# Hybrid SSD and short-convolution step: rows of x and B through VectorE transposes and DRAM, and a new order of the units in a group

## The chip, the cores and the metric

The kernel runs on one core of a Trainium2 chip. The metric is the time of one execution on the device in microseconds (us), as the median of three runs. Beside the timed runs there is one execution taken with the hardware profiler; its page and its trace are what is read here. Engines are named as in the profile: PE is TensorE (PEld its weight loads), DVE is VectorE, ACT is ScalarE, POOL is GpSimd, SP is SyncE, which here only issues DMAs.

## What is computed

One decoder layer for 336 tokens: 16 meta tokens and 256 prompt tokens in one sequence, and eight sample sequences of eight tokens. Cut to what matters here:

```
h = rms_norm(x);  proj = h @ w_in            # 2048 columns in, z | x,B,C | dt | four short-conv parts | two gates
x, B, C = silu(causal_conv4(proj[x,B,C]))    # x: 64 heads of 64; B, C: 8 groups of 128
cb = einsum('bcign,bcjgn->bcijg', C, B)      # per chunk of tokens i, j and group g
wts = cb[..., None] * decay * dt
y  = einsum(wts, x) + einsum(C, h_in) * exp(acum) + d_skip * x
chunk_states = einsum('bcjgr,bcjgrp,bcjgn->bcgrpn', to_end, x, B)    # then carried from chunk to chunk
y  = grouped_rms_norm(y * silu(z));  y_a = y @ w_ssd_out
y_b = (sc_b * conv3(sc_c * sc_h) * silu(sc_z)) @ w_sconv_out
out = x + (sigmoid(g_a) * y_a + sigmoid(g_b) * y_b) @ w_o            # then a final rms_norm
```

Everything is float32. The outputs are the normed tokens and the new convolution and scan states.

## The kernel before

Activations lie transposed: a tile has 128 features on the partitions and the tokens along the free axis. To keep float32 precision every operand of a large product is split into a high and a low part (`whi`, `wlo` for weights, `hhi`, `hlo` for activations, `yh`, `yl` for the scan's output), and a product is three matmuls: high by high (L111), high by low (L112) and low by high (L115), in `mm`. `wblk` (L90 to L97) loads 128x1024 weights into `wraw` by a DMA on SP's queue (L92), makes `whi` on ScalarE (L94) and `wlo` on VectorE (L96); each of the three tiles has three buffers. A unit is one 128-wide output tile with its two weight blocks (`unit`, `proj`), or, in `out_units`, one weight block for two output tiles. The result stands in a PSUM tile `pj`, of which there are two, until ScalarE or VectorE has emptied it.

The first part of the kernel does the short convolution branch and prepares tables (`dtt`, `act`, `tet`, decays and so on). The last part is the output projection. Between them stand eight groups g of the SSD branch, each of eight heads. Four kinds of units belong to a group:

- `conv_units` (L481 to L494): the projection and convolution of B, of C and of four x tiles. `conv_tile` (L457 to L479) copies `pj` into a padded tile on ScalarE (L462, L463), mends the sequence borders on POOL (L464 to L466), and convolves in the tile `cacc` (L469 on ScalarE, three times L471 on VectorE, L474 on ScalarE, L475 and L476 on VectorE). They are run one group ahead, for g+1.
- `z_units` (L496 to L506): four projections of z, emptied by ScalarE (L502, L503).
- `out_units` (L733 to L745): eight units of y @ w_ssd_out, run one group behind, for g-1. Each unit's two tiles are added into `ya` by VectorE (L744); for g = 0 ScalarE copies them (L742).
- `gate_units` (L747 to L763): the gates, four of them in group 0, four in group 7, the rest behind.

The scan itself, `ssd(g, st)`, is a generator with 24 steps. Its chunks c are 128, 128 and 80 tokens. `rows(c)` (L530 to L552) brings what the scan needs with tokens on the partitions: four TensorE transposes of the x tiles (L534) and one of B (L536) into PSUM, the C.B product (L537), then xdt = rows of x times dt (L539), the high and low part of B's rows (L546, L547; L542 for c = 2), and the masked C.B product `cbm` (L551). `decay` and `weights` make the matrix W from the table rows in DRAM (loaded at L527), the masked product and xdt; `halve`, `carry` and `state` carry the state; step 13 multiplies W by xdt (L650) and collects the scan's output in `ys`; later steps multiply by z (L673), take the group norm (L698 to L705), update the sample states (`h`, L713, L716, written back at L719) and scale `ys` and split it into yh and yl (L726 to L728).

`weave` (L775 to L786) sets the order. It goes through the units in the order of `parts`, each with a weight, and after each unit advances `ssd` so far that the 23 steps spread evenly over the weights. Program order is priority: the instructions of a step stand after those of the unit before them, and `behind` holds them, on ScalarE, VectorE and TensorE, behind the latest weight split or matmul of that unit. The compiler then arranges each engine's queue by this priority and by when it expects operands to be ready. Before, a group's order is z (4 units of weight 2), the output units of g-1 (8 of weight 1), the gates in groups 0 and 7 (4 of weight 2), and the convolutions of g+1 (6 of weight 2).

Two buffers limit the order. The tile `free` (L517), which holds B's rows of chunk 1 and the split xe, takes the slot that the x tiles of g+1 are written to later. And `yh`, `yl` have one buffer each, which the output units of g-1 read; `zq` (L692) uses yh's slot.

Of the kernel before, what the change touches and what calls it, by code (L numbers as in the profile page):

```python
# [1 line left out]

# [11 lines left out]
P = 128  # L14
T = 336
# [14 lines left out]
NSTEP = 23  # L30

# [16 lines left out]
def tile_hybrid_step(ctx, tc, xT, w0, w1, w2, wdt, wso, wsc, wo, cmask, vec, hvec, convst, sconvst, xe_, fwe, h0T,  # L48
# [13 lines left out]
    bq_d = [dr.tile([80, 4, P], F32, name=f"bq_d{i}") for i in range(2)]  # L62

# [26 lines left out]
    def wblk(src, n=1024):  # L90
        raw = wp.tile([P, 1024], F32, name="wraw")
        nc.sync.dma_start(raw[:, :n], src)  # L92
# [5 lines left out]

    def behind(tail):
        for ins in reversed(nc.cur_bb.bb.instructions):  # L100
            if ins is tail:
                break
            for a in latest.values():
                if ins.engine == a.engine:
                    tc.add_manual_dep(ins, a.name, mybir.DependencyInfo(mybir.DependencyClass.NoSync,
                                                                         mybir.DependencyReason.DATA), reason="step")
# [341 lines left out]
    with tc.tile_pool(name="pb", bufs=2) as pb:  # L448
# [8 lines left out]
        def conv_tile(src, j, t0, out, cs):  # L457
# [11 lines left out]
            nc.scalar.activation(acc[:, i0:], pad[:, i0:360], AF.Identity, bias=col(V_CB, j), scale=col(V_CW, 4 * j))  # L469
            for k in range(1, 4):  # L470
                nc.vector.scalar_tensor_tensor(acc[:, i0:], pad[:, i0 + k:360 + k], col(V_CW, 4 * j + k),  # L471
                                               acc[:, i0:], mult, add)
# [6 lines left out]
                acc[:, 272:360].rearrange("p (b t) -> p b t", t=11)[:, :, 3:11], add, mult)  # L479

        def conv_units(g, st):  # L481
            cs = pb.tile([P, 6, 9, 3], F32, name="cs")
            nc.sync.dma_start(cs, convst[:, g])
            BT = st["BT"] = pb.tile([P, T], F32, name="BT")
            conv_tile(w1[64 + g], 32 + g, 0, BT, cs[:, 4])
# [5 lines left out]
            for t in range(4):  # L491
                conv_tile(w1[32 + 4 * g + t], 4 * g + t, 0, xs[:, t, :], cs[:, t])
                yield
            nc.sync.dma_start(convo[:, g], cs)  # L494

        def z_units(g, st):  # L496
            st["zs"] = []
            for t in range(4):
# [4 lines left out]
                nc.scalar.activation(z[:, :TV], pz, AF.Copy)  # L503
                nc.vector.scalar_tensor_tensor(z[:, :TV], th, 1.0, z[:, :TV], add, mult)
# [9 lines left out]
        def ssd(g, st):  # L514
# [6 lines left out]
            W, xdt, xe, bt, cbm, hst = ([None] * 3 for _ in range(6))  # L521
# [8 lines left out]
            def rows(c):  # L530
                (t0, n), m = CH[c], NT[c]
                pp = ps.tile([P, 512], F32, name="ms")
                for t in range(4):
                    nc.tensor.transpose(pp[:n, t * P:t * P + P], xs[:, t, t0:t0 + n], ident)  # L534
                pq = ps.tile([P, 512], F32, name="ms")
                nc.tensor.transpose(pq[:n, 0:P], BT[:, t0:t0 + n], ident)  # L536
                nc.tensor.matmul(pq[:n, P:P + m], BT[:, t0:t0 + n], CT[:, TGT[c]:TGT[c] + m], start=True, stop=True)  # L537
                xdt[c] = big("xdt", 3)
                nc.vector.tensor_tensor(split(xdt[c][:n]), split(pp[:n]), bc(hv(dtt[:n, c, :], g), [n, 8, HP]), mult)  # L539
                if c == 2:  # L540
                    bt[c] = pb.tile([P, P], F32, name="bt", bufs=1)
                    nc.scalar.activation(bt[c][:n], pq[:n, 0:P], AF.Copy)  # L542
                else:
                    bt[c] = (free[:, 1024:1280].rearrange("p (i n) -> p i n", n=P) if c else
                             pb.tile([P, 2, P], F32R, name="bh0", bufs=1))
                    nc.scalar.activation(bt[c][:, 0, :], pq[:, 0:P], AF.Copy)  # L546
                    nc.vector.tensor_tensor(bt[c][:, 1, :], pq[:, 0:P], fb(bt[c][:, 0, :]), sub)  # L547
                cbm[c] = pb.tile([P, PX], F32, name="cbm")
                u0 = META if c == 0 else 0
# [486 lines left out]
```

## Time and profile before

| | us |
|---|---|
| median of 3 runs | 1823.05 (1822.67 to 1823.65) |
| the profiled execution | 1824.75, of which 1823.0 from the first to the last instruction |
| PE busy | 1814.9 |
| DVE busy | 1147.7 |
| ACT busy | 828.8 |
| POOL busy | 389.4 |

The granted TensorE clock is 1.00 throughout. The DMA engines moved 331.33 MB. In the timeline the groups begin after some 696 us and end at about 1645 us; a group in the middle takes 111.4 us. In rows of grouped instructions, the numbers behind the bar are the busy time in us, the mean length of one in ns, and then the engine's idle time just before them. In a timeline the first number is the start in us, the second the duration. A matmul's duration overlaps the next one's; the distance from start to start tells what it costs.

### The profile page before, as it was taken

The page shows a single profiled execution, that of the slowest core. Times are in us where ns is not written, and L with a number is a line of the kernel's source. Part 1 is how long each engine was busy: PE and PEld are TensorE (multiplying, and loading weights), DVE is VectorE, ACT ScalarE, POOL GpSimd, SP SyncE. Part 2 cuts the span into 40 slices and gives each one's busy share as a digit, 9 for nine tenths or more (in the row PEclk, how much of TensorE's full clock was granted, in tenths as well). Part 3 has the DMA queues.
Part 4 walks back from the last instruction along what each step waited for, and adds up shares of the span by engine and source line. Part 5 has one row for each costly group of instructions (what it writes and reads, how often), then busy time and mean ns, then how long its engine had stood idle before and what let it go on. Part 6 is the DMA issues. An engine that isn't in the chain of part 4 may idle for free.

```text
span 1823.0 us, 32410 instructions
## 1 busy us (share of the span) xinstructions
PE 1814.9 (100%) x13006; PEld 1798.0 (99%) x13006; DVE 1147.7 (63%) x1696; ACT 828.8 (45%) x1269; POOL 389.4 (21%) x398
## 2 busy tenths in 40 slices
PE   9999999999999999999999999999999999999998
PEld 9999999999999999999999999999999999999998
DVE  7745544444543335668587787877778777776544
ACT  6433333333333334645656354564546545343543
POOL 0000000000000001253162433524334252400012
PEclk9999999999999999999999999999999999999999
DMA  7444444444444446457566574665656657476553
GB/s 254 146 151 150 150 149 149 145 152 151 156 152 159 160 162 227 149 178 240 163 201 223 177 246 150 208 215 178 238 157 211 206 169 249 153 243 213 184 175 129
DMA packets 117286, 331.33 MB, mean 182 GB/s; under 512 B 20944, under 2 KB 37904, under 8 KB 117136
## 3 DMA queue, kind: packets, MB, share of 16 engines
q1 hardware_dynamic: 116272, 327.89, 55.9%
q8 instruction: 102, 1.67, 0.4%
q10 hardware_dynamic: 864, 1.38, 0.2%
q14 instruction: 48, 0.39, 0.1%
HBM read 296.34 MB, written 32.88 MB: 181 GB/s over the span
## 4 chain that ended last, share of the span: by engine, by line
PE 96%; DMA 2%; ACT 1%; DVE 1%; issue 0%; POOLq 0%; POOL 0%; SPq 0%; ACTq 0%; DVEq 0%
PE pj L111 30%; PE pj L112 30%; PE pj L115 29%; PE yb L650 2%; DMA wraw<-w 1%; PE ms L636 1%; PE pj L219 1%; PE yb L585 1%; PE pj L862 1%; ACT whi L94 0%; PE ms L534 0%; ACT W L559 0%; PE ms L219 0%; DMA ssms<-h 0%; PE yb L713 0%
## 5 line engine op out<-in xcount | busy, mean ns | idle before, releaser
L111 PE MATMUL pj<-hx,whi 128*128 128x320 f32 (+3 forms) x2880 | 864.4, 312 | 0.0
L112 PE MATMUL pj<-hx,whi 128*128 128x320 f32 (+3 forms) x2880 | 860.6, 311 | 0.0
L96 DVE TENSOR_TENSOR wlo<-wraw,whi 128x1024 fp32r<-128x1024 f32 x470 | 596.8, 1270 | 413.9 <-ACT whi L94 206.8
L94 ACT ACTIVATE whi<-wraw 128x1024 fp32r<-128x1024 f32 x470 | 496.7, 1057 | 768.0 <-PE pj L112 628.1
L111 PEld LDWEIGHTS pj<-hx,whi 128*128 128x128 f32 x2880 | 540.7, 188 | 4.6 <-ACT pad L462 1.7
L112 PEld LDWEIGHTS pj<-hx,whi 128*128 128x128 f32 x2880 | 541.5, 188 | 0.1
L115 PE MATMUL pj<-hx,wlo 128*128 128x320 f32 (+3 forms) x2880 | 485.4, 310 | 0.0
L115 PEld LDWEIGHTS pj<-hx,wlo 128*128 128x128 f32 x2880 | 440.6, 188 | 0.0
L111 PE MATMUL pj<-yh,whi 128*128 128x320 f32 x512 | 153.5, 311 | 1.2 <-ACT zs L503 0.9
L112 PE MATMUL pj<-yl,whi 128*128 128x320 f32 x512 | 152.3, 309 | 0.0
L596 POOL TENSOR_TENSOR h<-h,decS 128x512 f32<-128x512 f32 x64 | 76.4, 1227 | 147.5 <-PE ms L636 147.5
L111 PEld LDWEIGHTS pj<-yh,whi 128*128 128x128 f32 x512 | 96.2, 188 | 3.1 <-ACT zs L503 1.4
L112 PEld LDWEIGHTS pj<-yl,whi 128*128 128x128 f32 x512 | 96.3, 188 | 0.6
L115 PE MATMUL pj<-yh,wlo 128*128 128x320 f32 x512 | 95.8, 309 | 0.0
L242 POOL COPY SCS<-up 128x2 f32<-128x2 f32 x16 | 18.2, 1139 | 359.2 <-DVE up L236 329.0
L744 DVE TENSOR_TENSOR yan<-yan,pj 128x320 f32<-128x320 f32 x112 | 54.2, 485 | 62.9 <-PE pj L115 61.3
L471 DVE SCALAR_TENSOR_TENSOR cacc<-pad,V,cacc 128x360 f32<-128x360 f32 (+1 forms) x144 | 89.5, 621 | 2.0
L464 POOL COPY pad<-cs 128x24 f32<-128x24 f32 x48 | 56.2, 1172 | 126.6 <-DVE cacc L471 115.5
L115 PEld LDWEIGHTS pj<-yh,wlo 128*128 128x128 f32 x512 | 80.4, 188 | 0.0
L111 PE MATMUL pj<-vhi,whi 128*128 128x320 f32 x256 | 75.5, 308 | 0.0
L112 PE MATMUL pj<-vlo,whi 128*128 128x320 f32 x256 | 75.5, 308 | 0.0
L465 POOL COPY cs<-pad 128x3 f32<-128x3 f32 x48 | 45.0, 938 | 82.5 <-ACT pad L462 82.0
(286 smaller groups left out, 1721.7 us busy)
## 6 DMA issues: line engine op xcount, KB each, us to landing
wraw<-w SPq DMA_DIRECT2D x346, 512.0 KB, 3.9
wraw<-wso SPq DMA_DIRECT2D x64, 512.0 KB, 3.5
wraw<-wsc SPq DMA_DIRECT2D x32, 512.0 KB, 3.8
h<-h0T SPq DMA_DIRECT2D x32, 512.0 KB, 4.9
ssms<-h SPq DMA_DIRECT2D x32, 512.0 KB, 4.2
wraw<-wo SPq DMA_DIRECT2D x32, 512.0 KB, 3.9
xq_d<-xe SPq DMA_DIRECT2D x16, 320.0 KB, 3.4
W<-ac_d SPq DMA_DIRECT2D x8, 576.0 KB, 6.4
```

Of the source, the lines that this page charges most:

```text
L94: latest["act"] = nc.scalar.activation(hi[:, :n], raw[:, :n], AF.Copy).ins
L96: latest["dve"] = nc.vector.tensor_tensor(lo[:, :n], raw[:, :n], fb(hi[:, :n]), sub).ins
L111: nc.tensor.matmul(out, w, xh(k0 + k), start=first and k == 0, stop=False)
L112: nc.tensor.matmul(out, w, xl(k0 + k), start=False, stop=False)
L115: latest["pe"] = nc.tensor.matmul(out, w, xh(k0 + k), start=False, stop=last and k == nk - 1).ins
L219: nc.tensor.matmul(pu[i][:, :T - t0], w[:, o:o + P], x[:, k, t0:], start=k == 0 and j == 0, stop=k == 15 and j == 2)
L464: nc.gpsimd.tensor_copy(smp[:, :, 0:3], cs[:, 1:9, :])
L465: nc.gpsimd.tensor_copy(cs[:, 0, :], pad[:, 272:275])
L471: nc.vector.scalar_tensor_tensor(acc[:, i0:], pad[:, i0 + k:360 + k], col(V_CW, 4 * j + k), acc[:, i0:], mult, add)
L596: nc.gpsimd.tensor_tensor(split(h0[b]), split(h0[b]), bc(hv(decS[:, b, :], g), [P, 8, HP]), mult)
L650: nc.tensor.matmul(yb[q * HP:(q + 1) * HP, t, t0:t0 + n], x[:, h * HP:(h + 1) * HP], w[:, h, :], start=i == 0, stop=i == 3)
L744: nc.vector.tensor_tensor(ya[:, m, :TV], ya[:, m, :TV], pp[:, :TV], add)
```

## The change

Rows of x and B no longer come from TensorE. When a convolution tile of B or x is ready, VectorE transposes it in 32x32 blocks into the tile's own `cacc` buffer (320 columns, and the last 32 once more), and four DMAs, one for each 32 partitions, put the blocks into their places in a DRAM tile `xr_d[g % 2]` of 352 rows (tokens) by 640 columns (512 of x, 128 of B). The DMAs are issued on ScalarE's queue by `flush()`, which stands in the next unit, after ScalarE's first work there: in `conv_tile` behind L469, in `z_units` and in `out_units`. In `ssd`, step 2 issues loads of the rows into xdt and B's tile on SP's queue, eight DMAs for the three chunks, each behind the latest weight load; `rows_in(c)` multiplies xdt by dt in place and splits B, in steps 6, 7 and 9. The three C.B products stand together in `cross()`, in step 2. `decay(1)` goes from step 6 to 5.

The order of a group becomes z, B and C, two output units, the four x convolutions, six output units (and the gates last, in groups 0 and 7; in group 7 there are no convolutions, and eight output units follow z). For this, yh and yl are made behind the last unit of the weave instead of in step 21, `ys` is still scaled there, and `zq` uses E's slot.

```
+    xr_d = [dr.tile([XR, 640], F32, name=f"xr_d{i}") for i in range(2)]
...
+        pend = []
+        def flush():
+            while pend:
+                nc.scalar.dma_start(*pend.pop(0))
-        def conv_tile(src, j, t0, out, cs):
+        def conv_tile(src, j, t0, out, cs, rows=None):
...
+            flush()
...
+            if rows is not None:
+                nc.vector.transpose(acc[:, :320], out[:, :320])
+                nc.vector.transpose(acc[:, 320:XR], out[:, T - 32:])
+                to, c = rows
+                for a in range(0, P, 32):
+                    pend.append((to.rearrange("(b q) c -> q b c", q=32)[:, :, c + a:c + a + 32],
+                                 acc[a:a + 32, :XR].rearrange("p (b f) -> p b f", f=32)))
...
+            def load(c):
+                xdt[c] = big("xdt", 3)
+                b = bt[c] if c == 2 else fb(bt[c][:, 1, :])
+                rows = xr_d[g % 2]
+                for o, r, n in ((0, P * c, P),) if c < 2 else ((0, 256, 64), (64, 336, 16)):
+                    for d, q in ((xdt[c], slice(0, 512)), (b, slice(512, 640))):
+                        after(nc.sync.dma_start(d[o:o + n], rows[r:r + n, q]).ins, latest["sp"])
-            def rows(c):
-                for t in range(4):
-                    nc.tensor.transpose(pp[:n, t * P:t * P + P], xs[:, t, t0:t0 + n], ident)
-                nc.tensor.transpose(pq[:n, 0:P], BT[:, t0:t0 + n], ident)
-                nc.tensor.matmul(pq[:n, P:P + m], BT[:, t0:t0 + n], CT[:, TGT[c]:TGT[c] + m], start=True, stop=True)
...
+            def cross():
+                pq = ps.tile([P, 512], F32, name="ms")
+                qs = [pq[:n, o:o + m] for o, m, (_, n) in zip((0, NT[0], NT[0] + NT[1]), NT, CH)]
+                for c, (t0, n) in enumerate(CH):
+                    nc.tensor.matmul(qs[c], BT[:, t0:t0 + n], CT[:, TGT[c]:TGT[c] + NT[c]], start=True, stop=True)
...
+            def rows_in(c):
+                n = CH[c][1]
+                nc.vector.tensor_tensor(split(xdt[c][:n]), split(xdt[c][:n]), bc(hv(dtt[:n, c, :], g), [n, 8, HP]), mult)
+                if c < 2:
+                    b = fb(bt[c][:, 1, :])
+                    nc.scalar.activation(bt[c][:, 0, :], b, AF.Copy)
+                    nc.vector.tensor_tensor(bt[c][:, 1, :], b, fb(bt[c][:, 0, :]), sub)
...
-            zq = pb.tile([P, 4, TV], F32R, name="zq", tag="yh", bufs=1)
+            zq = pb.tile([P, 2, 576], F32R, name="zq", tag="E", bufs=1)[:, :, :TV]
...
             parts = [(z_units(g, S[g]), 4, 2)]
-            if g:
-                parts.append((out_units(g - 1, S[g - 1]), 8, 1))
+            out = out_units(g - 1, S[g - 1]) if g else iter(())
+            n, gate = 8 if g else 0, gate_units(4, 8) if g else gate_units(0, 4)
+            if g < NG - 1:
+                conv = conv_units(g + 1, S[g + 1])
+                first = min(n, 2)
+                parts += [(islice(conv, 2), 2, 2), (islice(out, first), first, 1), (conv, 4, 2)]
+                n -= first
+            parts.append((out, n, 1))
             if g in (0, NG - 1):
-                parts.append((gate_units(0, 4) if g == 0 else gate_units(4, 8), 4, 2))
-            if g < NG - 1:
-                parts.append((conv_units(g + 1, S[g + 1]), 6, 2))
+                parts.append((gate, 4, 2))
             weave(parts, ssd(g, S[g]))
```

More of the change, by code (lines that the diff above doesn't have):

```diff
@@ L1 @@
 from contextlib import ExitStack
+from itertools import islice
 import concourse.bass as bass
@@ L97, in wblk, with after @@
         return hi, lo
+    def after(ins, a):
+        tc.add_manual_dep(ins, a.name, mybir.DependencyInfo(mybir.DependencyClass.NoSync,
+                                                            mybir.DependencyReason.DATA), reason="step")
     def behind(tail):
@@ L102, in behind @@
                 break
[L103 to L106, printed above, removed]
+            for k in ("act", "dve", "pe"):
+                if k in latest and ins.engine == latest[k].engine:
+                    after(ins, latest[k])
     def mm(out, hi, lo, xh, xl, base, nk, k0, first, last):
@@ L520, in ssd @@
             ys = pb.tile([P, 4, T], F32, name="ys", bufs=1)
-            W, xdt, xe, bt, cbm, hst = ([None] * 3 for _ in range(6))
+            W, xdt, xe, cbm, hst = ([None] * 3 for _ in range(5))
             W[0], W[1] = (pb.tile([P, 8, PX], F32, name="W")[:, :, :n] for n in (P - META, PX))
@@ L528, in ssd @@
             NT, TGT = (P - META, PX, 80), (META, P, 2 * P)
-            def rows(c):
-                (t0, n), m = CH[c], NT[c]
-                pp = ps.tile([P, 512], F32, name="ms")
-                for t in range(4):
-                    nc.tensor.transpose(pp[:n, t * P:t * P + P], xs[:, t, t0:t0 + n], ident)
-                pq = ps.tile([P, 512], F32, name="ms")
[L536 to L549, printed above, removed]
-                for a, b, o in ((0, m, 0),) if c < 2 else ((META, 80, 0), (0, META, 64)):
-                    nc.vector.tensor_tensor(cbm[c][:n, o:o + b - a], pq[:n, P + a:P + b],
-                                            U[:, u0 + a:u0 + b] if c < 2 else UQ[:, a:b], mult)
@@ L598, in ssd @@
             yield
-            rows(0)
+            cross()
+            for c in range(3):
+                load(c)
             yield
@@ L603, in ssd @@
             nc.scalar.activation(E, W[1], AF.Exp)
-            rows(1)
             for u in range(4):
@@ L610, in ssd @@
             yield
+            decay(1)
+            yield
+            rows_in(0)
             weights(0)
@@ L613, in ssd @@
             halve(0)
-            decay(1)
-            yield
-            rows(2)
+            rows_in(1)
             yield
@@ L622, in ssd @@
             halve(1)
+            rows_in(2)
             decay(2)
@@ L726, in ssd @@
                         nc.vector.scalar_tensor_tensor(y, y, col(V_SNW, 4 * g + t), rs, mult, mult)
-                        nc.scalar.activation(yh[:, t, :], y, AF.Copy)
-                        nc.vector.tensor_tensor(yl[:, t, :], y, fb(yh[:, t, :]), sub)
-                    yield
+                yield
+            yh = pb.tile([P, 4, TV], F32R, name="yh", bufs=1)
+            yl = pb.tile([P, 4, TV], F32R, name="yl", bufs=1)
+            for t in range(4):
+                y = ys[:, t, META:]
+                nc.scalar.activation(yh[:, t, :], y, AF.Copy)
+                nc.vector.tensor_tensor(yl[:, t, :], y, fb(yh[:, t, :]), sub)
             st["y"] = (yh, yl)
```

23 lines of the change are left out of this document (17 added, 6 removed).

## The prediction

> **What bounds the kernel now.** I read the page first, then the list of waits of TensorE, the order of time of TensorE around one visit of the scan, and last VectorE, ScalarE and the DMAs in the stretches that the change rearranges. The page says how full TensorE (PE) is, and the list of waits says for whom it ever stood still:
>
> ```profile
> span 1823.0 us, 32410 instructions
> ## 1 busy us (share of the span) xinstructions
> PE 1814.9 (100%) x13006; PEld 1798.0 (99%) x13006; DVE 1147.7 (63%) x1696; ACT 828.8 (45%) x1269; POOL 389.4 (21%) x398
> ```
> ```profile
> PE pj L111 <- ACT zs L503: 0.9, 1, 0.9
> PE pj L827 <- POOL rs_r L823: 0.3, 1, 0.3
> PE pj L111 <- DVE yan L744: 0.3, 1, 0.3
> ```
>
> The columns of a wait are the sum in us, how often, and the longest. Busy PE spans overlap, so 100% alone proves little; that after its start TensorE waited only 1.5 us for others proves it: every matmul that goes is time won, as long as no new wait appears. In the weaves, no wait for a weight is on the list, though ScalarE's splitting of the weights is often late. Now one visit of the scan, `rows(0)` of the first group, instruction by instruction (start, duration):
>
> ```profile
> 752.12 0.60 PE L534 MATMUL ms<-CR,xs 128*128 128x128 f32 x4
> 752.55 0.27 PE L536 MATMUL ms<-CR,BT 128*128 128x128 f32 x1
> 752.66 0.37 PE L537 MATMUL ms<-CT,BT 128*128 128x112 f32 x2
> 752.80 0.40 PE L111 MATMUL pj<-hx,whi 128*128 128x320 f32 x1
> 753.04 0.31 PE L112 MATMUL pj<-hx,whi 128*128 128x320 f32 x1
> 753.19 0.31 PE L111 MATMUL pj<-hx,whi 128*128 128x320 f32 x1
> ```
>
> Durations overlap, so starts are read. The four transposes of x take 752.55 - 752.12 = 0.43 us, that of B 0.11, the C.B product 0.14. The first projection matmul after the visit holds its successor up for 0.24 us instead of the 0.15 that follows: returning costs 0.09.
>
> **Part 1, what leaves TensorE.** All transposes go; the three C.B products stay, in one visit instead of three.
>
> ```profile
> L534 PE MATMUL ms<-CR,xs 128*128 128x128 f32 (+1 forms) x96 | 14.4, 272 | 0.0
> ...
> L536 PE MATMUL ms<-CR,BT 128*128 128x128 f32 (+1 forms) x24 | 6.5, 272 | 0.0
> ```
>
> 96 = 24 visits of four, and 24 of B. The gain is 24 x (0.43 + 0.11) = 13.0 us, and two returns less in each of eight groups, 16 x 0.09 = 1.4: together **14.4 us**. It is all on the path, since PE is. The Trainium skill, "VectorE: DVE Perf Modes", section "Rules for kernel authors", speaks against the change: for a 128x128 transpose it says to use TensorE where a PSUM destination will do. That page puts one (in bf16) at 390 ns, by which 120 of them would be an estimated 46.8 us; the starts above show 0.11 us each and decide, and no row shows why a full TensorE should keep them.
>
> **Part 2, VectorE (DVE) and the order of the group.** Five convolution tiles of each group get two 32x32 transposes each. In steady state, for one whole group and for its heaviest DMA stretch:
>
> ```profile
> 955.00:983.00 28.00, 28.00 (x193) 27.54 (x193) 21.44 (x36) 14.01 (x23) 8.58 (x9) 1.00 0.82 275
> 955.00:1066.50 111.50, 111.50 (x840) 109.73 (x840) 87.33 (x136) 58.60 (x100) 42.77 (x42) 1.00 0.62 200
> ```
> ```profile
> L643 DVE STREAM_TRANSPOSE xe<-xe x8: 445/445/448, 800.6 to 1576.1; 128x256 f32<-128x256 f32 x8
> ```
>
> (The windows' columns are PE, weight loads, DVE, ACT, POOL, clock, DMA share, GB/s.) By 0.445 us for 256 columns, 320 take 0.56 and 32 at least 0.06, with a start of its own at most 0.2 (the estimate I use is 0.15); five tiles come to 3.6 us, and DVE goes from 87.3 to 91 us in a group of 109.7. It does not become the bound over a group. The multiplications of xdt and the splitting of B stay, with SBUF sources instead of PSUM, and I take them at the same price.
>
> Locally it is different. Now the eight output units stand in the middle of a weave, and the six convolutions at its end, where the steps are that use DVE most. Afterwards six output units stand there. Each of their two tiles must be added out of PSUM (L744) before the tile after next may start: `pj` has two buffers. The convolutions had no such hurry. The cadence today:
>
> ```profile
> 1013.98 0.49 DVE L744 TENSOR_TENSOR yan<-yan,pj 128x320 f32<-128x320 f32 x1 [1.27 <-PE pj L115]
> 1014.48 1.22 DVE L96 TENSOR_TENSOR wlo<-wraw,whi 128x1024 fp32r<-128x1024 f32 x1
> 1015.74 0.49 DVE L744 TENSOR_TENSOR yan<-yan,pj 128x320 f32<-128x320 f32 x1
> ```
>
> Two adds and one `wlo` per unit, 2 x 1.76 = 3.52 us. Six units last 21.1 us and need 12 x 0.49 + 6 x 1.22 = 13.2; 7.9 us are left. What else falls there (counts in this view are those of the last 20 us of today's weave):
>
> ```profile
> L471 DVE SCALAR_TENSOR_TENSOR cacc<-pad,V,cacc 128x360 f32<-128x360 f32 x7 | 4.1, 588 | 0.0
> L716 DVE TENSOR_TENSOR h<-h,yb 128x1024 f32<-128x1024 f32 x2 | 2.4, 1218 | 0.0
> L726 DVE SCALAR_TENSOR_TENSOR ys<-ys,V,ms_r 128x320 f32<-128x320 f32 x4 | 2.1, 544 | 0.0
> L728 DVE TENSOR_TENSOR yl<-ys,yh 128x320 fp32r<-128x320 f32 x4 | 1.9, 483 | 0.0
> L703 DVE SCALAR_TENSOR_TENSOR ms_a<-ms_r,ms_x 128x320 f32<-128x320 f32 x2 | 1.0, 488 | 0.0
> ...
> L475 DVE SCALAR_TENSOR_TENSOR xs<-cth,cacc 128x272 f32<-128x272 f32 x2 | 0.9, 434 | 0.0
> ```
>
> By the weights of the weave (28, with 23 steps), after the last x convolution come step 18 (the group norm, L701 to L705), 19 and 22 (two h updates each) and 21 (the scaling of ys). With the last x tile's own work that is 3 x 0.59 + 0.43 + 0.7 of transposes, 7 x 0.49, 4 x 1.22 and 4 x 0.54: 13.4 us for 7.9. So 5.5 us too much in 21. Some of it slides into the next z units, where DVE has room, as today's tail already does. What comes ahead of an add costs PE time once the add is over 1.76 - 0.49 - 0.31 (the last matmul's tail) = 0.96 us late. The trace has one such event, in the last weave, with ScalarE as the late engine (it empties the z units' PSUM, L502 and L503):
>
> ```profile
> 1547.56 2.12 ACT L559 ACTIVATE W<-W,act 80x80 f32<-80x80 f32 x8
> 1549.71 0.74 ACT L562 ACTIVATE W<-W 80x640 f32<-80x640 f32 x1
> 1550.36 1.04 ACT L94 ACTIVATE whi<-wraw 128x1024 fp32r<-128x1024 f32 x1
> 1551.31 0.41 ACT L502 ACTIVATE cth<-pj 128x320 f32<-128x320 f32 x1
> ```
>
> Work of the steps ran ahead of L502, and PE stood 0.9 us. Bounds for a weave's six-unit tail: 0, if adds always slip in, and 5.5 us, if all the excess goes first. I take **1.5 us**: a pair of h updates ahead of an add (2 x 1.22 - 0.96 = 1.5), close to the event seen. It counts in weaves 2 to 6, five times, **7.5 us** in all. Weave 1 empties by ScalarE (g == 0), weaves 0 and 7 have no such tail.
>
> **Part 3, the way through DRAM.** Per group 20 writes on ScalarE's queue (four a tile, 352 pieces of 128 bytes each, 0.90 MB) and eight loads on SP's (0.86 MB).
>
> ```profile
> 1817.46 0.34 ACTq L926 DMA_DIRECT2D yE<-yt  x1
> ```
> ```profile
> W<-ac_d SPq DMA_DIRECT2D x8, 576.0 KB, 6.4
> xh<-xq_d SPq DMA_DIRECT2D x16, 256.0 KB, 4.4
> W<-ac_d SPq DMA_DIRECT2D x8, 448.0 KB, 5.7
> ```
> ```profile
> ACT whi L94 <- DMA wraw<-w: 76.7, 28, 5.7
> ```
>
> Four issues hold ScalarE for 4 x 0.34 = 1.4 us, 6.8 per group; behind them wait `whi` splits and PSUM copies. They are issued one unit after the transposes, so they should not wait. The cover is the lead of the split weights: ScalarE came up to 5.7 us late 28 times because of a DMA, and no PE wait followed. The loads go out at step 2, behind the latest weight load, and delay the next ones by 0.86 MB at 275 GB/s = 3.1 us, in the stretch that is 82% full. I take both at nothing; without cover the loads would cost 3.1 us in seven groups, 22 us. The new DVE wait for a load (`rows_in`, step 6; behind it stand `wlo` and the adds) comes four steps of 111.5 / 23 = 4.8 us after the issue, 19 us against landings of 4 to 6. The 448 KB load has 1,024 pieces, the 576 KB one 128, and lands no later: the number of pieces hardly matters, and 0.90 MB by bytes is 3.3 us a group, whose DMA share is 0.62 on average. zq in E's buffer waits for two transfers issued two steps before, which land within that time. yh and yl, moved behind the last unit, have six projection units until they are read, but for weave 7, where the last gate unit (48 matmuls at 0.15, 7 us) covers 4 x 0.48; uncovered it would be 2 us, once.
>
> **Sum.** -14.4 + 7.5 + 0 = -6.9. The profiled execution took 1824.75 us, 1.7 above the median of the three runs, so the profile of after should be at 1817.9 and the median at 1823.05 - 6.9 = **1816.2**. A change under 0.2%, 3.6 us, I count as none: that is about what a measurement here can tell.
>
> **Rivals.** First, nothing is lost: the adds slip between the steps' instructions, which depend on each other in chains. For it: in the present output stretches PE waited 0.3 us on L744 in all, with step work between the adds there too. Against: those stretches leave DVE idle time and the tail does not. 1823.05 - 14.4 = 1808.7 (up to 1811).
>
> Second, **the other side**: in the six-unit tail the excess goes ahead of the adds. Place: L111 of the second tile after a late L744, steps 18 to 22. Price: up to 5.5 us in five weaves, 27.5 us, 1836.2. It eats the gain from 2.9 us a weave; from 2.2 us the result is within 0.2%, from 3.6 us slower. For it speaks that the tail is overfull and that early-traced steps went first in the event above; against it, that steps which nothing waits for can slide into the z units.
>
> Third, small pieces clog the DMA engines: if 128 bytes cost as much as an average packet, the group does not fit.
>
> ```profile
> q1 hardware_dynamic: 116272, 327.89, 55.9%
> ```
>
> That is 0.559 x 1823 x 16 / 116272 = 0.14 us a packet, 7,040 pieces 62 us of every engine in a group whose engines already work 0.62 x 111.5 = 69: 131 us for 109.7, 21 us more in seven groups, 1956 us. Weights come late from about 0.09 us a piece. The 448-byte row speaks against it, though it reads DRAM and does not write it. The Trainium skill, "DMA: Bandwidth & Descriptors", section "Specifications", states that line rate needs 512 bytes, and that below this the DMA engine does a read-modify-write; no run so far shows 128-byte writes.
>
> **How the numbers follow.** Forecast, 0.5 to 2.1 us a weave lost (1811 to 1819.4): 0.52. Nothing lost: 0.15. The tail takes 2.2 to 3.6 us a weave, within 0.2%: 0.15. Over 3.6: 0.12. Clogged DMAs or late weights: 0.06. Faster 0.67, same 0.15, slower 0.18. The range is 1808.5 to 1828: below it almost nothing, above it half of the fourth case and the fifth.
>
> **What would show it.** Right: L534 and L536 gone, 16 returns fewer, PE waits on L744 or starts of L111 about 1 us late near the ends of weaves 2 to 6, some 7 us together; no PE wait on `whi`. Wrong: PE waits on DVE sums under 2 us (first rival) or over 14 (second); landings of `wraw` over 6 us with ScalarE waiting on them (third). Part 1 would be wrong if, with the visits gone, the projection's cadence of 0.15 us a matmul rose.

## The result and the profile after

The changed kernel takes 1851.8 us (median of 4 runs, 1850.9 to 1854.7) against 1823.0 (1822.7 to 1823.7): 1.016 times as long, interval 1.0143 to 1.0178, **28.7 us slower**. The forecast was 1816.2. The profiled execution took 1850.9 us.

Line numbers are now those of the changed kernel: `whi` L97, `wlo` L99, matmuls L117, L118, L121, the writes of rows L467, `pad` L474 and L475, the adds L779. The page's line of busy times, then the waits of TensorE (sum, times, longest in us):

```profile
PE 1813.3 (98%) x12886; PEld 1787.6 (97%) x12886; DVE 1202.4 (65%) x1776; ACT 825.6 (45%) x1261; POOL 356.7 (19%) x398
```
```profile
PE pj L117 <- DVE yan L779: 11.8, 17, 1.2
PE pj L117 <- ACT pad L475: 9.4, 11, 2.2
PE pj L117 <- ACT yan L777: 4.9, 3, 3.6
PE pj L121 <- DVE wlo L99: 1.9, 1, 1.9
...
PE pj L117 <- ACT whi L97: 0.7, 1, 0.7
```

29 us of waits after the warm-up, where there were 1.5. The list starts to count at the modelled end of the last matmul; by the distances from start to start PE lost about 38 us more than before. The saving is there as well. One visit of the scan holds all that is left of 16.7 us of transposes and C.B products:

```profile
1215.82 0.77 PE L567 MATMUL ms<-CT,BT 128*128 128x112 f32 x6
1216.39 0.39 PE L117 MATMUL pj<-hx,whi 128*128 128x320 f32 x1
```

It costs 1216.39 - 1215.82 = 0.57 us; over the eight groups the visits fell from 16.7 to 4.8 us (both from start to start), and 16 returns of 0.09 us went: **13.4 us gained**. Three places show how more than that was lost.

**The junction of C and the first output units** (group 3). C's last matmul and what ScalarE (ACT) does then:

```profile
1130.10 1.35 PE L121 MATMUL pj<-hx,wlo 128*128 128x324 f32 x8
...
1133.87 0.41 PE L117 MATMUL pj<-yh,whi 128*128 128x320 f32 x1 [0.66 <-ACT pad L475]
```
```profile
1130.55 1.05 ACT L97 ACTIVATE whi<-wraw 128x1024 fp32r<-128x1024 f32 x1
1131.93 1.34 ACTq L467 DMA_DIRECT2D xr_d<-cacc  x3
1133.32 0.39 ACT L474 ACTIVATE pad<-pj 128x260 f32<-128x260 f32 x1 [1.72 <-PE pj L121]
```

C is complete at 1131.45 and ScalarE is free at 1131.60, but three writes of B's rows stand ahead in its queue. They wait for VectorE's transposes and are issued from 1131.93 to 1133.27. Only then is `pj` emptied, and PE has stood. The bracket blames PE; the row above it shows the cause.

**The tail of weaves 2 to 6** (weave g is the one that runs beside group g's scan), here weave 3, first on VectorE (DVE), then the matmul of PE that waits:

```profile
1184.53 0.68 DVE L617 TENSOR_TENSOR hst<-hst,ms 128x512 f32<-128x512 f32 x1
1185.13 0.48 DVE L736 SCALAR_TENSOR_TENSOR ms_a<-ms_r,ms_x 128x320 f32<-128x320 f32 x1
1185.53 1.22 DVE L749 TENSOR_TENSOR h<-h,yb 128x1024 f32<-128x1024 f32 x1
1186.66 0.48 DVE L737 TENSOR_TENSOR ms_a<-ms_a,ms_r 128x320 f32<-128x320 f32 x1
1187.06 1.21 DVE L749 TENSOR_TENSOR h<-h,yb 128x1024 f32<-128x1024 f32 x1
1188.19 0.48 DVE L738 SCALAR_TENSOR_TENSOR ms_r<-ms_a,ms_r 128x320 f32<-128x320 f32 x1
1188.60 0.48 DVE L779 TENSOR_TENSOR yan<-yan,pj 128x320 f32<-128x320 f32 x1
```
```profile
1189.22 0.39 PE L117 MATMUL pj<-yh,whi 128*128 128x320 f32 x1 [1.15 <-DVE yan L779]
```

The add comes behind six step instructions, and PE's next output tile starts 1.31 us late, counted from start to start. With its neighbours (0.70, 0.14, 0.66, 0.47) such a tail loses **3.28 us**, about the same in each of the five. The 0.70 of it is not a wait for an add: there PE waits for ScalarE's copy of the last x tile (`pad` L475).

**Weave 1**, where ScalarE empties the output tiles (g = 0):

```profile
947.66 0.50 ACT L487 ACTIVATE cth<-cacc 128x360 f32<-128x360 f32 x1 [2.23 <-DVE cacc L484]
948.18 1.28 ACT L733 ACT_TABLE_LOAD   x1
949.45 0.36 ACTq L467 DMA_DIRECT2D xr_d<-cacc  x1
...
949.85 0.48 ACTq L467 DMA_DIRECT2D xr_d<-cacc  x1
949.90 0.75 ACT L777 ACTIVATE yan<-pj 128x320 f32<-128x320 f32 x2
```

The two copies come at 949.90, behind ScalarE's wait for the convolution on VectorE and a table load; PE lost 3.8 us here. Transfers did not clog (DMA queues: packets, MB, share of 16 engines' span; issues: KB each, us to landing):

```profile
q10 hardware_dynamic: 59744, 8.60, 2.7%
```
```profile
wraw<-w SPq DMA_DIRECT2D x346, 512.0 KB, 3.9
wraw<-wso SPq DMA_DIRECT2D x64, 512.0 KB, 4.6
...
xr_d<-cacc ACTq DMA_DIRECT2D x160, 44.0 KB, 2.5
```

Before, `w` landed in 3.9 us as well, `wso` in 3.5. ScalarE's waits for weights grew from 76.7 us (28 waits) to 118.8 (52), but only 0.7 us of that reached PE, as the list above shows.

### The profile page after: what moved, and what is told of

Its sections match the earlier page's. It is cut to its first block, busy times and chain, and to the rows that moved or that the text cites. A ratio compares the mean times of both kernels' runs of the same rounds, so it can differ in the third digit from the quotient of the medians.

```text
span 1849.1 us, 32601 instructions
## 1 busy us (share of the span) xinstructions
PE 1813.3 (98%) x12886; PEld 1787.6 (97%) x12886; DVE 1202.4 (65%) x1776; ACT 825.6 (45%) x1261; POOL 356.7 (19%) x398
## 3 DMA queue, kind: packets, MB, share of 16 engines
q10 hardware_dynamic: 59744, 8.60, 2.7%
## 5 line engine op out<-in xcount | busy, mean ns | idle before, releaser
L117 PE MATMUL pj<-hx,whi 128*128 128x320 f32 (+3 forms) x2880 | 862.9, 312 | 2.5 <-DVE yan L779 1.6
L118 PE MATMUL pj<-hx,whi 128*128 128x320 f32 (+3 forms) x2880 | 860.4, 311 | 0.0
L99 DVE TENSOR_TENSOR wlo<-wraw,whi 128x1024 fp32r<-128x1024 f32 x470 | 590.9, 1262 | 375.8 <-PE pj L121 200.5
L97 ACT ACTIVATE whi<-wraw 128x1024 fp32r<-128x1024 f32 x470 | 493.8, 1056 | 703.7 <-PE pj L118 496.4
L117 PEld LDWEIGHTS pj<-hx,whi 128*128 128x128 f32 x2880 | 540.6, 188 | 6.4 <-issue 3.5
L118 PEld LDWEIGHTS pj<-hx,whi 128*128 128x128 f32 x2880 | 541.5, 188 | 0.3
L121 PE MATMUL pj<-hx,wlo 128*128 128x320 f32 (+3 forms) x2880 | 485.6, 310 | 1.9 <-DVE wlo L99 1.9
L121 PEld LDWEIGHTS pj<-hx,wlo 128*128 128x128 f32 x2880 | 440.5, 188 | 2.2 <-DVE wlo L99 2.2
L117 PE MATMUL pj<-yh,whi 128*128 128x320 f32 x512 | 158.2, 321 | 24.4 <-DVE yan L779 10.3
L118 PE MATMUL pj<-yl,whi 128*128 128x320 f32 x512 | 153.4, 311 | 0.0
L117 PEld LDWEIGHTS pj<-yh,whi 128*128 128x128 f32 x512 | 97.2, 190 | 36.3 <-ACT pad L475 12.7
L484 DVE SCALAR_TENSOR_TENSOR cacc<-pad,V,cacc 128x360 f32<-128x360 f32 (+1 forms) x144 | 107.4, 746 | 18.8 <-ACT cacc L481 15.1
L118 PEld LDWEIGHTS pj<-yl,whi 128*128 128x128 f32 x512 | 97.4, 190 | 0.3
L121 PE MATMUL pj<-yh,wlo 128*128 128x320 f32 x512 | 95.6, 310 | 0.0
L121 PEld LDWEIGHTS pj<-yh,wlo 128*128 128x128 f32 x512 | 80.7, 189 | 0.0
L117 PE MATMUL pj<-vhi,whi 128*128 128x320 f32 x256 | 75.5, 308 | 0.0
L118 PE MATMUL pj<-vlo,whi 128*128 128x320 f32 x256 | 75.5, 308 | 0.0
L600 POOL TENSOR_TENSOR E<-E,CT 128x1152 f32<-128x1152 f32 x8 | 24.7, 3091 | 253.4 <-ACT E L635 253.4
L487 ACT ACTIVATE cth<-cacc 128x360 f32<-128x360 f32 (+1 forms) x48 | 24.1, 502 | 92.4 <-DVE cacc L484 92.4
L779 DVE TENSOR_TENSOR yan<-yan,pj 128x320 f32<-128x320 f32 x112 | 53.0, 481 | 16.5 <-PE pj L121 14.8
```

The lines of the kernel that those rows point to most:

```text
L97: latest["act"] = nc.scalar.activation(hi[:, :n], raw[:, :n], AF.Copy).ins
L99: latest["dve"] = nc.vector.tensor_tensor(lo[:, :n], raw[:, :n], fb(hi[:, :n]), sub).ins
L117: nc.tensor.matmul(out, w, xh(k0 + k), start=first and k == 0, stop=False)
L118: nc.tensor.matmul(out, w, xl(k0 + k), start=False, stop=False)
L121: latest["pe"] = nc.tensor.matmul(out, w, xh(k0 + k), start=False, stop=last and k == nk - 1).ins
L487: nc.scalar.activation(th[:, i0:], acc[:, i0:], AF.Tanh)
```

## The experiments

The first theory (A) was that the new order of units makes all these stalls. Its rival (B): the rows' way through VectorE and DRAM makes them. Each run stands against the kernel before on the same chip (1823.2 to 1824.1). The compiler arranges the queues anew for every variant, so differences of 1 to 2 us between variants prove little, and a new arrangement can bring a wait of its own, as in e3 and e8. e7, e8 and e12 leave work out, as said below, so they do not compute the layer; they are there for their times alone.

| run | us | against before, us |
|---|---|---|
| e1 old order, rows through DRAM | 1881.9 | +58.3 |
| e2 new order, rows by TensorE | 1828.1 | +4.5 |
| e3 all steps ahead of the tail | 1870.0 | +46.4 |
| e4 eight output units, then x | 1882.6 | +59.0 |
| e5 writes on SP | 1850.2 | +27.0 |
| e6 writes on POOL | 1837.8 | +14.5 |
| e7 no writes (groups 1 to 7) | 1827.4 | +4.2 |
| e8 no transposes | 1854.5 | +31.2 |
| e9 three buffers of cacc | 1847.4 | +23.9 |
| e10 writes on POOL, three cacc | 1834.7 | +11.2 |
| e11 as e10, old order | 1873.6 | +50.1 |
| e12 no writes, no transposes | 1822.4 | -1.1 |
| e13 as e9, issued a unit later | 1849.8 | +25.7 |
| e14 as e10, issued a unit later | 1835.0 | +10.9 |
| e15 as e11, loads two steps later | 1872.0 | +47.9 |
| e16 as e2, with three idle loads | 1828.8 | +4.7 |
| e17 as e11, loads on POOL too | 1851.5 | +27.9 |
| e18 as e10, loads on POOL too | 1837.6 | +14.0 |

**Order or rows.** e1 puts the old list of `parts` into the changed kernel, e2 the new one (with the moved yh, yl and zq) into the kernel before. In e3 and e4 one line of the changed kernel differs:

```
e3: -            parts.append((out, n, 1))
    +            parts.append((out, n, 0 if 0 < g < NG - 1 else 1))
e4: -                first = min(n, 2)
    +                first = n
```

> The changed kernel with one part undone: the units of a group stand again in the order z, eight output units, six convolutions. The rows of x and B still go through VectorE's transposes and DRAM, C.B is still one visit, yh and yl still come last. Two theories of the 28.7 us by which the changed kernel is slower. A, the order: matmuls wait because output units, which come every 3.9 us or so and are added by VectorE one by one, now stand where VectorE and ScalarE are busy with steps or with a convolution; the rows through DRAM cost no time. Then the 13.4 us that the trace of the changed kernel shows saved on TensorE come out whole: 1823.0 - 13.4 = 1809.6, 1807 to 1814. B, the rows: the transposes on VectorE, the 160 issues on ScalarE's queue and the loads delay those two engines, whatever the order: at least half of the loss stays, 1838 or more.

> The kernel before with one part of the change added: the new order of the units (z, B, C, two output units, four x convolutions, six output units), with yh and yl made last and zq in E's buffer, which that order needs. Rows still by TensorE transposes, in three visits with C.B. Theory A (the order costs the time): the stalls that grew by about 38 us in the changed kernel come here without the saving, 1823 + 38 = 1861, at least 1848. Theory B (the rows through VectorE and DRAM cost it): 1821 to 1828.

> The changed kernel, but in groups 1 to 6 the six output units at the end count nothing in the spreading of the steps: all 23 steps are issued by the last x convolution, and the six output units run with no step between them (steps stand closer ahead of that). Theory A: the 3.28 us that PE waits in each of the five tails (16.4 us) go for the most part, and with closer steps some 3 us come back elsewhere: 1851.8 - 16.4 + 3 = 1838, 1833 to 1844. Theory B: the work of VectorE and ScalarE is the same in sum and only stands earlier, so no gain: 1849 to 1856.

> The changed kernel with all eight output units after B and C and the four x convolutions last (z, B, C, eight output units, x), where the change has two of them there and six at the end. Theory A, in its narrow form (the tail): the 16.4 us of the five tails go, since the steps that end there now stand beside convolutions, which come only every 6 us or so; the wait at the junction of C and the first output units stays (8.4 us), and about half of the 10.5 us of the first two weaves: 1851.8 - 16.4 - 5 = 1830, 1820 to 1836. Theory B: 1846 or more.

All four went against A. The new order alone costs 4.5 us, and with rows through DRAM the old order is among the worst. B holds, though e3 took 14 us more than the range that B had for it. What PE waited for, first in e1, then in e2:

```profile
PE pj L117 <- ACT whi L97: 37.6, 19, 5.2
```
```profile
PE pj L112 <- DVE yan L747: 3.4, 5, 0.7
```

In e1 the weights come late, and SP's queue shows why:

```profile
1219.95 0.33 SPq L503 DMA_DIRECT2D cs<-convst  x1
1225.71 1.92 SPq L561 DMA_DIRECT2D xdt<-xr_d  x4
1227.73 0.84 SPq L95 DMA_DIRECT2D wraw<-w  x2
```
```profile
SPq L561 <- DMA xr_d<-cacc: 49.3, 10, 7.9
```

The loads of rows wait at the head of SP's queue until the last x tile's write has landed, the weight loads wait behind them, and PE stood from 1230.3 to 1234.2. With the x tiles last (e1, e4) the write is issued beside the first z unit; the six output units behind the x tiles are what keeps this wait out of the changed kernel. e3 failed in another way: with the steps closer together, PE waited 26.1 us for `wlo`.

**Which part of the rows.** e5 and e6 change the issuing queue, e7 writes group 0's rows only and loads them in every group, e8 takes the two transposes out.

```
e5: -                nc.scalar.dma_start(*pend.pop(0))
    +                nc.sync.dma_start(*pend.pop(0))
e6: +                nc.gpsimd.dma_start(*pend.pop(0))
e7: -                for a in range(0, P, 32):
    +                for a in range(0, P, 32) if to is xr_first[0] else ():     # group 0 alone
e8: -                nc.vector.transpose(acc[:, :320], out[:, :320])
    -                nc.vector.transpose(acc[:, 320:XR], out[:, T - 32:])
```

> The changed kernel with the 160 row writes issued on SP's queue instead of ScalarE's. After the first four runs: the order alone cost 4.5 us, so the rows cost the rest, 1851.8 - 1828.1 = 23.7 us in the new order, and with the 13.4 us saved on TensorE some 37 us are lost to them. Three theories for it. C, ScalarE's queue: a write waits for VectorE's transposes, and what stands behind it on ScalarE (the copies out of pj, whi) waits with it; four issues take 1.4 us besides. Then this kernel wins most of it back: 1815 to 1832. D, VectorE: its added work (0.67 us of transposes a tile, xdt now multiplied from SBUF in 1.17 instead of 0.68 us) makes adds and wlo late; then nothing changes here, 1846 to 1856. E, SP and the DMAs: the loads of rows stand ahead of weight loads, and writes on SP make that worse: 1855 or more.

> The changed kernel with the 160 row writes issued on POOL's queue instead of ScalarE's. C (ScalarE's queue): 1815 to 1835, unless POOL's own work (the sample states' decay, the borders of the convolutions) gets as late by it. D (VectorE): 1846 to 1856. E (SP and the DMAs): no change either, 1848 to 1856.

> The changed kernel without the row writes of groups 1 to 7: their tiles are still transposed, but only group 0's rows go to DRAM, and every group loads those. It leaves out 140 of the 160 issues and the waits of the loads for them. C (ScalarE's queue): at most 1828, as far as 1812 if nothing else is lost. D (VectorE): 1842 to 1852. E (the loads on SP): if it is their waiting for writes, as C; if it is their transfer ahead of the weights, 1842 to 1852.

> The changed kernel without the 80 transposes of VectorE: the writes carry untransposed values, everything else stays. It takes 27 us of work from VectorE and two instructions from the chain between a convolution and its write. D (VectorE): most of the loss goes, 1818 to 1832. C (ScalarE's queue): the writes are ready 0.67 us earlier and the four issues stay, 1838 to 1850. E (the loads): 1846 to 1854.

By the ranges alone e7 fits C, e5 fits D, e6 lies between C and D, and e8 lies above all three of its ranges; the waits have to tell more. The writes are the price: without them the loss against before falls by 24.5 us, and by 14.2 when they only move from ScalarE to POOL. On SP they only change whom PE waits for: `whi`, 17.2 us in 14 waits, because weight loads now stand behind them (SP stood 95.7 us in writes that waited for transposes). D falls as the main cause by e7, which keeps every transpose and still wins 24.5 us. e8 proves less than it seems to. Its waits for adds and for `pad` are down to 2.4 and 1.4 us, but another one has taken their place:

```profile
PE pj L121 <- DVE wlo L99: 21.0, 5, 4.2
```

Once in each of weaves 2 to 6, `wlo` now stands behind the group norm and two h updates in VectorE's queue. So e8 does not say what the transposes cost; e12 below does, for a kernel without writes. e6's waits:

```profile
PE pj L117 <- DVE yan L779: 11.7, 15, 1.2
...
PE pj L117 <- ACT pad L475: 1.9, 3, 1.2
PE pj L117 <- ACT yan L777: 1.5, 2, 1.0
```

Against the changed kernel the two rows of ScalarE fell from 14.3 to 3.4 us, and that of VectorE's adds stayed (11.8 and 11.7). At C's end in group 3 nothing stands any more between `whi` and the copy out of `pj`:

```profile
1123.11 1.05 ACT L97 ACTIVATE whi<-wraw 128x1024 fp32r<-128x1024 f32 x1
1124.06 0.37 ACT L474 ACTIVATE pad<-pj 128x260 f32<-128x260 f32 x1
```

**What of a write.** A third cacc buffer finds room with one buffer of cs and b3 in bt's slot.

```
e9:  -            acc = pb.tile([P, 360], F32, name="cacc")
     +            acc = pb.tile([P, 360], F32, name="cacc", bufs=3)
e10: e9 + writes on nc.gpsimd        e11: e10 + the old list of parts
e12: e7 + transposes of group 0 only
```

> The changed kernel with three buffers of cacc instead of two (room for it: one buffer of cs, and b3 in bt's slot). So far: without the writes 24.4 us less, with the writes on POOL's queue 14.1 less, on SP's no change, without the transposes no change. Two theories of what a write costs. C1, the issue: on ScalarE, four issues and their wait for VectorE hold up the pj copies and whi behind them; then a third buffer changes little, 1846 to 1854. C2, the buffer: cacc is now given back only when its write has landed (issue in the next unit, then 2.5 us), and the convolution after next waits for it on ScalarE (12.6 us of ScalarE's waits name a write's landing); then 1832 to 1842.

> Both at once: row writes on POOL's queue and three buffers of cacc. With the writes left out the time was 1827.4, which is the floor for any way of issuing them. C1 (the issue on ScalarE): as POOL's queue alone, 1834 to 1839. C2 (the buffer): 1827 to 1833. A third, C3, the transfers themselves (7,040 pieces of 128 bytes a group beside the weights' loads) would leave 1836 or more here and in the run before 1846 or more.

> As the run before, row writes on POOL's queue and three buffers of cacc, but with the units in the order of the kernel before (z, eight output units, six convolutions). In that order, with the writes on ScalarE, the time was 1881.9, and the loads of rows stood 49 us on SP waiting for writes to land, with weight loads behind them (PE then waited 37.6 us for whi). If that wait is of the order (the last x tile's write is issued beside the first z unit and the load for it two steps later), the time stays over 1860 here. If the wait was of ScalarE's late issues, it goes: 1825 to 1840.

> The changed kernel with neither the row writes nor the transposes of groups 1 to 7: every group loads group 0's rows. What is left of the new path are the loads, the multiplication of xdt from SBUF, and C.B in one visit. The kernel before in the new order took 1828.1; the 13.4 us saved on TensorE would make that 1814.7, and with transposes but no writes it was 1827.4, 12.7 more. D (VectorE's transposes cost that): 1814 to 1818. E (the loads cost it): 1824 to 1828.

The buffer is worth 3 to 5 us, less than C2 said. In e10 PE's remaining waits are mostly for adds (11.7 us). In e11 the wait stays: 47.6 us of SP for writes, 41.8 us of PE for `whi`. e12 lies between its two theories: transposes cost 5.3 us (e7 less e12), and 7.8 remain above the ideal of -8.9 (4.5 for the order less the 13.4 saved).

**Delay, place and queue of the transfers.**

```
e13 (on e9), e14 (on e10): flush() issues what the flush before it found, and stands in gate_units too
e15 (on e11):  -            cross(); for c in range(3): load(c)             # step 2
               +            (step 4, ahead of the h0 loads) for c in range(3): load(c)
e16 (on e2):   +            for c in range(3):
                   nc.sync.dma_start(ys.rearrange("p t n -> p (t n)")[:, 512 * (c % 2):512 * (c % 2) + 512], h0T[g, :, c, :])
e17 (on e11), e18 (on e10): -    after(nc.sync.dma_start(d[o:o + n], rows[r:r + n, q]).ins, latest["sp"])
                            +    nc.gpsimd.dma_start(d[o:o + n], rows[r:r + n, q])
```

> Three buffers of cacc, row writes on ScalarE's queue as in the change, but each tile's four writes are issued one unit later still, so that VectorE's transposes are long done when ScalarE comes to them. Writes on ScalarE with three buffers took 1847.4, on POOL 1834.7. C1a, ScalarE's loss is its wait in order for the transposes: 1833 to 1839. C1b, it is the issues' own time (four of some 0.35 us a tile, 56 us in all): 1844 to 1849.

> The same delay with the writes on POOL's queue, where POOL waited 63.4 us for the transposes. If POOL's wait, which holds the convolutions' border copies behind it, is what is left of the writes' price (1834.7 against 1827.4 without writes): 1828 to 1832. If it is the transfers, or the loads' wait for them: 1833 to 1837, or more where the later write makes a load wait.

> Old order, writes on POOL, three buffers of cacc, and the row loads issued two steps later, in step 4 ahead of the h0 loads. With the loads in step 2 it took 1873.6, and SP stood 47.6 us on loads waiting for writes, weight loads behind them; PE waited 41.8 us for whi. If that wait is the price of the old order, it goes with the later loads: 1873.6 - 41.8 = 1832, 1822 to 1842. If the old order is bad for another reason: 1860 or more.

> The kernel before in the new order (1828.1) with three loads of 256 KB a group added on SP's queue in step 2, where the change has its row loads; they read the initial states into ys, which is overwritten later, so they cost only as transfers and issues. E (the loads cost the 7.7 us by which the kernel without writes and transposes, 1822.4, stays above 1828.1 - 13.4 = 1814.7): 0.75 of 0.82 MB, so about 7 us more, 1833 to 1838. Otherwise the 7.7 us belong to VectorE's operations that now read SBUF and to C.B in one visit: 1827 to 1830.

> Old order, three buffers of cacc, row writes and now the row loads too on POOL's queue, loads again in step 2. Moving the loads by two steps on SP left SP's waits for writes at 41.3 us: SP runs ahead of the units, so its loads still came before the last write had landed (in one group SP stood from 1216.5 to 1222.0 before the loads of xdt, the next weight load was issued at 1224.0, and PE stood 4.9 us from 1225.5). With the loads on POOL no weight load stands behind that wait. If it is the price of the old order, PE's 41 us of waits for whi go: 1873.6 - 41.8 = 1832, and less if VectorE has more room in that order, 1816 to 1838. If the old order is bad for another reason: 1860 or more.

> The same in the new order: writes and loads on POOL, three buffers of cacc (with the loads on SP 1834.7). There SP hardly waited for a row write, so the loads' queue should make no difference: 1831 to 1838. If loads ahead of weight loads on SP cost time even so: 1826 to 1830.

e13 and e14 do not decide between the theories they were made for, because the delay did not take hold. In e13 the first write of 31 of the 40 tiles still starts 0.03 us after the tile's transposes end; in the changed kernel it is 36 of 40. One tile of e13, VectorE and then ScalarE, which had been free since 1176.84:

```profile
1179.67 0.17 DVE L497 STREAM_TRANSPOSE cacc<-xs 128x32 f32<-128x32 f32 x1
```
```profile
1179.87 1.90 ACTq L467 DMA_DIRECT2D xr_d<-cacc  x4
```

On POOL the waits for transposes are 64.2 us in e14 against 63.4 in e10. How much of ScalarE's 14.2 us is its waiting for transposes and how much the issues' own time therefore stays open. The issues are not small. In the changed kernel (ns, least, median and most):

```profile
L467 ACTq DMA_DIRECT2D xr_d<-cacc x160: 309/475/2472, 707.5 to 1528.9; - x160
```

The 160 together are 74 us, put between ScalarE's other work. e16: three loads a group that nothing waits for cost nothing (0.2 us), so E falls as far as it is the transfers. e15 did not remove SP's wait (41.3 us): SP runs ahead of the units, and two steps were too few. e17 does, by taking the loads off the weights' queue (and out of their place behind the latest weight load); PE's waits:

```profile
PE pj L117 <- DVE yan L779: 16.7, 5, 3.4
...
PE pj L117 <- ACT whi L97: 3.4, 4, 1.5
```

`whi` went from 41.8 to 3.4 us and the time fell by 22, not by 41: another wait takes over, adds of the output units that stand behind a step's work on VectorE, five times and up to 3.4 us. In e18, where there was no such wait to remove, the queue of the loads won nothing (2.8 us more than e10). So SP's wait makes some 22 of the 39 us by which e11 is slower than e10; with all transfers on POOL the old order still costs 14 us more than the new (e17, e18), and that rest was not taken apart.

No variant that computes everything beat the kernel before.

## Why the prediction was wrong

The measured sum: the saving on TensorE -13.4 (from the trace), the new order +4.5 (e2), what e12 leaves beyond these two, reading rows from SBUF and the rest of the new steps, +7.8, transposes +5.3 (e7 - e12), writes in any queue +10.3 (e6 - e7), writes on ScalarE's queue +14.2 (after - e6). Together +28.7. The sum closes because each term starts where the one before ends; a term holds in that sequence, and taken out in another one (the transposes alone in e8) it can be worth something else.

- **Part 1 held.** 14.4 predicted, 13.4 measured. C.B in one visit costs 0.60 us, not 3 x 0.14.
- **Part 3 is the step that failed.** "They are issued one unit after the transposes, so they should not wait ... I take both at nothing." For the loads this was right in the new order (e16, e18). For the writes it cost 24.5 us (after - e7). They did wait: 36 of 40 tiles' first writes start 0.03 us after their transposes end. The text priced the issues (1.4 us a tile; by the median of 0.475 it is 1.9) and took the lead of `whi` as the cover. But copies out of `pj` stand on ScalarE as well, and they have no lead: two buffers, and an output tile that takes 1.76 us. Four issues with the wait ahead of them are about as long as that. The cover was looked for in the wrong instruction. This goes with the 14.2 us that are won when ScalarE no longer issues (its two rows of waits fall by 10.9 of them); the other 10.3 are in part open (below).
- **Part 2, the tail**: the mechanism was right, the size was not. 1.5 us a weave predicted, 3.28 measured (0.70 of it for `pad`), 16.4 in all, beyond the break-even of 2.9 that the second rival named. Yet e2 has the same tail and loses 0.84 us a weave from start to start, 3.4 in all by its list of waits. The excess of VectorE's work alone therefore did not do it; with the order alone the 7.5 us foreseen were even too much, and it took the rows' path as well. ScalarE in weave 3 of e2, then of the changed kernel:

```profile
1162.46 0.40 ACT L463 ACTIVATE pad<-pj 128x272 f32<-128x272 f32 x1 [0.16 <-PE pj L116]
...
1164.29 0.53 ACT L701 ACTIVATE ms_r<-ms,eps 128x320 f32<-128x320 f32 x1
```
```profile
1177.34 0.38 ACT L474 ACTIVATE pad<-pj 128x272 f32<-128x272 f32 x1
...
1183.06 0.53 ACT L733 ACTIVATE ms_r<-ms,eps 128x320 f32<-128x320 f32 x1
```

  The group norm's `ms_r` followed the last x tile's copy by 1.8 us and now follows it by 5.7, and VectorE's steps after it stand among the h updates. That is where the adds come late here, but not all of why: in weave 3 of e6 the distance is 1.8 us again (1167.55 to 1169.35), and over the run its adds cost as much. Run by run, PE's waits for adds are 3.4 us (e2), 5.9 (e12, with the reading of rows), 8.9 (e7, with transposes as well) and 11.7 (e6, with writes as well): each part of the path goes with some 3 us, even with no write on ScalarE.
- **Same price from SBUF**: the price taken for xdt's multiplication was right in 17 of 24; seven took 1.79 us instead of 0.68 (last section).
- **Not foreseen at all**: the junction of C and the first two output units (4.9 us in weaves 2 to 6) and weaves 0 and 1 (10.5 us, 2.1 of them for `wlo` in weave 0), counted at nothing because "Weave 1 empties by ScalarE". ScalarE was just the engine that the change loaded.
- **Third rival**: small pieces did not clog. 2.7% of 16 engines' span over 59744 packets is 13 ns each, a tenth of the 0.14 us assumed for it, and `wraw` lands in 3.9 us as before. The Trainium skill, "DMA: Bandwidth & Descriptors", "Specifications", has a read-modify-write below 512 bytes; no run here takes its cost apart, and what share the transfers have in the 10.3 us of writes on any queue is open. The same page of the Trainium skill, "Issuing engines are not separate DMA queues", calls the time that a sequencer takes to start a DMA usually small relative to the DMA itself; here an issue took 0.475 us against 2.5 to landing, and the choice of the issuing engine made 14 us.
- **The Trainium skill's rule against the change** ("VectorE: DVE Perf Modes", "Rules for kernel authors": TensorE for a 128x128 transpose if PSUM will do as destination) was set aside because a full TensorE seemed the only price. The runs side with the rule: 13.4 us on TensorE were dearer to move than to pay. Most of the loss came from the way through DRAM, not from VectorE's transposes (5.3 us).

Open: the 7.8 us of e12. Of them 4.7 stand in PE's list of waits (adds 5.9 and ScalarE's copies 2.2, against 3.4 in e2). A candidate is VectorE's work on rows that now come from SBUF (below); no run isolates it. The 10.3 us of writes on any queue are split only in part: 3.3 of them go with a third buffer (e10), 2.8 stand in the waits for adds (11.7 in e6, 8.9 in e7), and whether these overlap and what the rest is was not tried.

## What to carry to other kernels

Before an engine with slack is given DMA issues, look at what stands behind each issue in its queue, and count the issue time against the buffer with the fewest spares there, not against the average load. Where an experiment delays or moves something, see in its trace that it moved before its time is read: e13, e14 and e15 left the wait in place that they were to remove. A load that waits for a store holds everything behind it on the issuing queue, so a round trip through DRAM needs either a queue without urgent loads or a unit's worth of other work between store and load. Cutting work on the full engine pays only what the helpers' timing leaves of it: 13.4 us saved here cost 42.1 elsewhere.

## What the runs showed of the hardware

**A wait of some 4 us slows TensorE afterwards.** In e1 the five stalls of 3.5 to 5.5 us are each followed by 11 to 20 matmuls at half speed (windows: PE, weight loads, DVE, ACT, POOL, clock, DMA share, GB/s):

```profile
1228.00:1234.00 6.00, 2.46 (x17) 2.20 (x16) 0.14 (x2) 0.90 (x1) 0.00 (x0) 0.93 0.91 290
1234.00:1236.00 2.00, 1.79 (x7) 1.79 (x8) 1.73 (x2) 1.76 (x5) 0.00 (x0) 0.50 0.18 72
1236.00:1240.00 4.00, 4.00 (x17) 4.00 (x17) 3.77 (x5) 4.00 (x12) 1.82 (x1) 0.50 0.71 225
1240.00:1246.00 6.00, 6.00 (x42) 6.00 (x42) 5.22 (x5) 5.44 (x13) 2.87 (x2) 1.00 0.33 116
```

From start to start a matmul here takes 0.27 us for some 6 us, then 0.15 again: some 21 matmuls by 0.12, 2.6 us more. e1's mean clock is 0.989, that of the changed kernel 0.997 (the 3.8 us of weave 1 did the same there), that of the kernel before 1.000. The Trainium skill, "TensorE: Matmul & The Clock Gate", "Part 1", describes this: half rate after an idle window of about 3.4 us. The trace agrees for these five. Shorter stalls had no one outcome: in e1 two of 2.8 and 3.0 us were followed by 14 slow matmuls each, a third of 2.9 by one, and in e8 a wait of 1.9 us (at 744.9) by 13, at a clock of 0.53.

**VectorE beside POOL.** Three convolution instructions that take 1.85 us elsewhere in this trace took 4.17 while POOL worked on SBUF for 1.04 + 1.28 = 2.32 us, which is the difference:

```profile
1125.94 4.17 DVE L484 SCALAR_TENSOR_TENSOR cacc<-pad,V,cacc 128x360 f32<-128x360 f32 x3
```
```profile
1126.17 1.04 POOL L609 TENSOR_TENSOR hst<-hst,cdec 128x512 f32<-128x512 f32 x1
1127.17 1.28 POOL L604 TENSOR_TENSOR xw<-xe,xw 128x512 fp32r<-128x512 f32 x1
```

Such meetings belong to the new order rather than to the rows: the mean of this line is 0.62 us before, 0.84 in e2 and 0.75 here. For xdt's multiplication it is the rows. From PSUM it took 0.68 us every time, in e2 too, where POOL worked beside 13 of the 24. From SBUF (ns, least, median and most):

```profile
L578 DVE TENSOR_TENSOR xdt<-xdt,dtt x24: 674/679/1798, 759.9 to 1578.0; 128x512 f32<-128x512 f32 x16, 80x512 f32<-80x512 f32 x8
```

Seventeen still take 0.68 us; the seven that take 1.79 are those beside which POOL makes `xw`. The Trainium skill, "SBUF — State Buffer", section "SBUF: two separate sides", says that VectorE with two SBUF inputs and POOL lock each other out of a shared port. These rows fit it; no run varied POOL's work by itself.
